# Two reorderings in a two-layer trunk: retention's rotary and gate items alternate, and the down projections scale the second half's residual rows in products four and five

## The chip, the cores and the metric

The kernel runs on one core of a Trainium2 chip. The metric is the device time of one execution in microseconds. An execution is also recorded by the hardware profiler; its rows give engine, source line, tiles, start and length of each instruction. PE is the matrix engine (TensorE), DVE the vector engine (VectorE), ACT ScalarE, POOL GpSimd, and SP the engine that only issues DMAs here.

## The reference

The input x has 1024 rows of 1024 numbers. Two layers follow each other, with different mixers, and only the structure matters here:

```python
for i in range(2):
    mod = (e @ ada_w[i] + ada_b[i])[:, None, :]
    sh1, sc1, g1, sh2, sc2, g2 = jnp.split(mod, 6, axis=-1)
    y = mixers[i](x * (1 + sc1) + sh1)        # layer 0: gated deltanet, layer 1: retention
    x = layer_norm(ALPHA * x + (1 + g1) * y, ln_g[i, 0], ln_b[i, 0])
    y = conv_ffn(x * (1 + sc2) + sh2, ...)    # (silu(conv(gate)) * up) @ w_down, width 2816
    x = layer_norm(ALPHA * x + (1 + g2) * y, ln_g[i, 1], ln_b[i, 1])
```

Retention projects h to q, k, v and a gate; q and k are rotated by position (rotary), v is mixed over chunks, and the result is multiplied by silu(gate). `layer_norm` is a standardisation and then `* ln_g + ln_b` by column; this last step is called "the gain" below.

## The kernel before, in words

**Numbers.** Each operand of a matmul is split into a rounded high part and a rest (`split`, lines 88 to 90: an ACT copy at L89, a DVE subtraction at L90), and each product is three matmuls: high by high and the two cross terms (L110 to L112, L285 to L287, L1163, L1437).

**Halves.** The 1024 rows are two halves of 512, each of four row tiles of 128 rows; columns are two halves of 512 as well. A row tile of 128x1024 is loaded by `load_row` (L280).

**Strassen.** The large projections use seven products of half-size blocks in place of eight. In the up direction (`strassen`, L1157) a list of *items* is worked through one after the other; each gives four output blocks to a `sink`. An item's weight blocks must be split by ACT and DVE (L89, L90) before PE reaches it. In the retention layer the items are gate items (`gate_item`, L1663: one ACT silu per block at L1667 and a DMA) and rotary items (`rope_item`, L1639: six DVE operations of 128x512 for each of two column halves, L1651 to L1656, and four DMAs on ACT's queue). Before the change the order is two gate items, eight rotary items, six gate items. The value projection (`ret_v`, L1685) comes next.

**Down projections.** `proj_gen` (L1274) makes the feed-forward's down projection, once in each layer. Its seven products p = 0 to 6 (A blocks 11, S1, S2, S4, 12, S3, 22) each have eleven steps of 12 matmuls, so some 30 us each. At each step the A block `ar` (L1270) and the B block (`Bw` or `Br`, L1303) come by SP's queue and are split (`ab`, `bb`).

**Residual rows.** The residual rows of the second FFN sum are `gain(standardised rows)`. The standardised rows lie in a DRAM scratch (`xs`), without the gain. For the first half `xload(0, t)` (L1348) loads a row tile at p = 2 and DVE applies the gain there. For the second half `gain_half` (L1339 to L1346) prepares the rows beforehand: SP loads a 128x512 piece (L1343), GpSimd multiplies it by ln_g and adds ln_b (two operations, L1345), and GpSimd's own queue stores it to a second scratch `xg` (L1346). There are eight such pieces for each down projection: four row tiles by two column halves. `xload(1, t)` (L280) then loads the four row tiles from `xg` in product five's hooks.

**Buffers.** `xload` and `gain_half` take their SBUF tiles from the same tag, "lane", which has four slots of 4 KB for each partition (L43); so does a rotary item's scratch, and the pieces of `bg_gain` (L393, L394), which applies the gain of another row set on GpSimd in the background. A slot is free again when the last reader of its tile is done. The first half's four row tiles are in these slots from p = 2 on, until `finish` (L1357 to L1361: scale, add, statistics) and `norm` (L1363 to L1382) are through. In layer 0 they are then standardised (L294), transposed (L266) for the next layer and stored to scratch (L370); in layer 1 they are multiplied by the final gain (L1377 to L1381) and stored to the output by SP (L1379, L1382). The second half goes the same way after product seven; in layer 0 its transposes are L421. Each row tile's `norm` has one tiny GpSimd operation, the power of -0.5 (L1368).

**Order.** The program text doesn't fix the order of instructions. A list scheduler with a model of durations places each operation and each buffer, from the dependencies and the order in which the generators yield; the result is one fixed sequence for each engine and each DMA queue, which runs in order on the chip. Background work such as `bg_gain` is put in where slots and engines are free.

Of the kernel before, what the change touches and what calls it, by code (L numbers as in the profile page):

```python
# [22 lines left out]
RH = 4  # L23
# [10 lines left out]
def trunk_kernel(ctx: ExitStack, tc, A):  # L34
# [47 lines left out]
    def hs(half):  # L82
        return slice(half * HALF, (half + 1) * HALF)
# [322 lines left out]

    def build_T(B, xts, scale, shift, tags):
        tags = dict(zip(("T1", "T2", "T3", "T4", "22"), tags))
        tags["12"] = tags["T1"]
        for nm in tags:  # L410
            B[nm] = [None] * 4

        def put(nm, k, src, eng=dve):
            t = two(tags[nm], F32R, nm)
            split(t[0], t[1], src, eng)
            B[nm][k] = t

        def load(f, tag):
            pt = mm_tile()
            for t in range(4):  # L420
                pe.transpose(pt[:, t * P:(t + 1) * P], xts[t][:, f * P:(f + 1) * P], ident)  # L421
            tmp = tl(tag, [P, HALF], name="bt")
            act.activation(tmp, pt, AF.Identity, bias=shift[:, f:f + 1], scale=scale[:, f:f + 1])
            return tmp

        raw = []
        for k, tg in enumerate((("qkv", "qkv"), ("qkv", "qkv"), ("t2", "t2"), ("t2", "ada"))):
            b12, b22 = load(k, tg[0]), load(4 + k, tg[1])
            put("12", k, b12, pool if BAL["b3"] & 1 << k else dve)
            put("22", k, b22, pool if BAL["b2"] & 1 << k else dve)  # L430
            raw.append((b12, b22))

        one = tl("S", [P, P], F32R, name="one")
        act.activation(one, ident, AF.Copy)

        def whole(b, k):
            pt = mm_tile()
            for i, x in enumerate(B[b][k]):
                pe.matmul(pt, one, x, start=(i == 0), stop=(i == 1))
            return pt  # L440

        def rest():
            for k in range(4):
                t1, b22 = raw[k]
                x11 = whole("11", k)
                dve.tensor_sub(b22, b22, t1)
                put("T3", k, b22, pool if BAL["b3"] & 1 << k else dve)
                dve.tensor_add(b22, b22, x11)
                put("T2", k, b22, pool if BAL["bT"] & 1 << k else dve)
                dve.tensor_sub(t1, t1, x11)  # L450
                put("T1", k, t1, pool if BAL["b1"] & 1 << k else dve)
                dve.tensor_sub(b22, whole("21", k), b22)
                put("T4", k, b22)

        return rest
# [701 lines left out]
    def strassen(hT0, xts, scale, shift, items, tags=("hTb", "hTb", "qkv", "qkv", "aux"), direct=False):  # L1157
        B = {"11": hT0[:4], "21": hT0[4:]}
        nblk = [0]
# [7 lines left out]
        def side(n, s):  # L1167
            out = []
            for u in items[n][:2]:
# [4 lines left out]
                for i, b in enumerate((("11", "21"), ("12", "22"))[s]):  # L1174
                    for k in range(4):
                        mm3(X, w, k + 4 * i, B[b][k], i == 0 and k == 0, i == 1 and k == 3)
                out.append(X)
# [96 lines left out]
    def proj_gen(nj, ablk, wsrc, slots, xsrc, G, final, ln_next, tag, ltags, dst, key, mm=pe.matmul, gate=None, gain=None):  # L1274
# [64 lines left out]
        def gain_half(n):  # L1339
            hf, rs = n // 4, slice(HALF + n % 4 * P, HALF + (n % 4 + 1) * P)  # L1340
            x = tl("lane", [P, HALF], name="xg")
            with after("w"):
                sp.dma_start(x, gain[1][rs, hs(hf)])  # L1343
            for r, op in zip(grows, (ALU.mult, ALU.add)):
                pool.tensor_tensor(x, x, r[hf], op)  # L1345
            pool.dma_start(xsrc[rs, hs(hf)], x)  # L1346
# [100 lines left out]
        for p, (an, bn, fin, side, fresh) in enumerate(prods):  # L1447
            if gate and p < 2 or banks[side] is None:
                banks[side] = acc4() if gate and p < 2 or side == 0 else [sc_tile(), sc_tile(), mm_tile(), mm_tile()]
                if gate and p == 1:  # L1450
                    banks[0] = banks[1]
                    banks[1] = None
            accs = banks[0] if gate and p == 1 else banks[side]
            tail = []
            depth = ltags[3] if p == 6 else 2
            for j in range(nj):
                if gate and p < 2:
                    yield gate(j)
                    yield from take("qkv", 2)
                    give("qkv", 2)  # L1460
                a, w = ops(an, bn, j, not gate and p < (7 if final else 5))
                with after("a"):
                    for st in steps[p * nj + j + ahead:p * nj + j + ahead + 1]:
                        load_b(*st)
                if gain and p < 2 and j % 2 == 0 and p * 4 + j // 2 < 8 and j < 8:
                    gain_half(p * 4 + j // 2)
                if gain and p == 2 and j % 2 == 0 and j < 8:
                    xload(0, j // 2)
                if p == 2 and j < 4 and gate:
                    xload(0, j)  # L1470
                    finish(0, j, 0, c11[j])
                if j >= nj - depth:
                    tail.append((j, a, w))
                else:
                    for t in range(4):
                        mma(accs[t], t, a, w, fresh and j == 0, False, mm if p < 2 else pe.matmul if fresh else mm_on)
                        yield 0.0
                for _ in range(-(-20 // (nj - 1)) if p == 6 else 4 if p == 5 else 2):
                    if later:
                        later.pop(0)()  # L1480
                if p == 5 and j > 1 and not later:
                    for _ in range(-(-16 // (nj - 2))):
                        if hooks:
                            hooks.pop(0)()
                bg_step()
            while later:
                later.pop(0)()
            if p == 5:
                while hooks:
                    hooks.pop(0)()  # L1490
            if p == 6:
                pin[0] = None
            for t in range(4):
                for j, a, w in tail:
                    mma(accs[t], t, a, w, fresh and j == 0, j == nj - 1, mm if p < 2 else pm_on if p == 6 else pe.matmul if fresh else mm_on)
                fin(t, accs[t])
                yield 0.0
            if p == 1:
                yield "P2"
            if p == 4:  # L1500
                hooks = [] if final else ln_hooks(0, xts[0], tag, ln_next, outs, dst, key, bal["h"])
                hooks += [lambda t=t: xload(1, t) for t in range(4)]
# [106 lines left out]
    def next0():  # L1609
        if not fbox:  # L1610
            while bg or pend:
                bg_step()
            fbox["f"] = fold(1, 0, 1)
        return fbox["f"]
# [24 lines left out]
    def rope_item(h, j):  # L1639
        def start():  # L1640
            c = {}

            def sink(q, a, b):
                c[q] = c_of(q, a, b)
                hf = q % 2
                if hf not in c or hf + 2 not in c:
                    return
                x1, x2 = c[hf], c[hf + 2]
                cos, sin = trig(h, j)
                m = tl("lane", [P, 2, HALF], name="rm")  # L1650
                dve.tensor_mul(m[:, 0], x2, sin[hf])  # L1651
                dve.tensor_mul(m[:, 1], x1, sin[hf])
                dve.tensor_mul(x1, x1, cos[hf])
                dve.tensor_mul(x2, x2, cos[hf])
                dve.tensor_sub(x1, x1, m[:, 0])
                dve.tensor_add(x2, x2, m[:, 1])  # L1656
                for d, x in enumerate((x1, x2)):
                    act.dma_start(qd[j, h, d][:, hs(hf)], x)
            return sink
        u = 8 * j + 2 * h  # L1660
        return A["ret_wqk"][u], A["ret_wqk"][u + 1], start, None

    def gate_item(u):  # L1663
        def start():
            def sink(q, a, b):
                c = c_of(q, a, b) if b is not None else tl("cv", [P, 516], name="sg")[:, 0:HALF]
                act.activation(c, a if b is None else c, AF.Silu)  # L1667
                act.dma_start(gd[u + q // 2][:, hs(q % 2)], c)
            return sink
        return A["ret_wg"][u], A["ret_wg"][u + 1], start, None  # L1670

    sc_r, sh_r = next0()
    B = strassen(h0, xts, sc_r, sh_r, [gate_item(0), gate_item(2)]
                 + [rope_item(h, j) for h in range(RH) for j in range(2)] + [gate_item(u) for u in range(4, 16, 2)], ("hTa", "aux", "qkv", "qkv", "hTa"), True)
    hT = [h0, []]
    xlo = []
    for t in range(4):
# [271 lines left out]
```

## Time and profile before

| | |
|---|---|
| median of 3 runs | 2971.46 us (2971.45 to 2976.05) |
| span of the profiled execution, first to last instruction | 2967.8 us |
| mean granted TensorE clock in it | 0.985 |
| PE, DVE, ACT, POOL busy | 2820.5, 2242.4, 1316.5, 474.8 us |
| layer 0's down projection | about 1200 to 1427 us |
| retention's items | about 1427 to 1745 us |
| layer 1's down projection | about 2731 to 2949 us, then normalising and output to 2967.8 |

The profiled execution's whole time is not shown beside its span; the span lies 3.66 us below the median of the runs. A row of a timeline reads: start in us, length in us, engine, line, operation, out<-in, tile and types, count, and in brackets how long the engine had been idle before and what ended that. In a table of stretches each engine's busy time stands with its instruction count in parentheses. A row of waits reads: engine, tile and line that waited, <- who ended the wait, then total us, number of times, and the longest.

### The profile page before, as it was taken

To read this page: it belongs to the slowest core of one execution; us is meant where nothing else is said; L and a number is where in the kernel's file an instruction comes from. 1 tells how busy PE (TensorE), PEld (TensorE's weight loads), DVE (VectorE), ACT (ScalarE), POOL (GpSimd) and SP (SyncE) were. 2 spreads that over 40 slices of the span, in tenths; PEclk is the share of its full clock that TensorE was granted. 3 is DMA by queue.
4 is the path that set the end of the run, shared out by engine and by line. 5 is a ranking of instruction groups with operands and counts; after the bars stand their busy time and mean duration, and the time that the engine had idled before them with its cause. 6 is when DMAs were issued, how large, how long until landed. Compare 5 with 4: busy or idle time off the path is not lost. (4 is left out here: it accounts for less than half of the span.)

```text
span 2967.8 us, 38939 instructions
## 1 busy us (share of the span) xinstructions
PE 2820.5 (95%) x13638; PEld 2304.5 (78%) x13638; DVE 2242.4 (76%) x4005; ACT 1316.5 (44%) x2413; POOL 474.8 (16%) x469
## 2 busy tenths in 40 slices
PE   8999898999999999999999999999999999999997
PEld 7887777887788888787877887777777788887786
DVE  5787787656688888879678645666689887777979
ACT  4744564444544444446433442222344544444443
POOL 0312221100001111610000202322202011112301
PEclk9999999999999999999999999999999999999998
DMA  7231222254245445865333544665664243335753
GB/s 275 79 113 65 86 79 79 83 167 160 91 158 163 158 151 174 305 198 179 120 128 117 181 160 152 203 189 175 205 212 157 91 135 107 107 107 176 274 183 137
DMA packets 244404, 451.01 MB, mean 152 GB/s; under 512 B 23088, under 2 KB 76592, under 8 KB 244208
## 3 DMA queue, kind: packets, MB, share of 16 engines
q1 hardware_dynamic: 213088, 401.07, 41.0%
q10 hardware_dynamic: 29760, 43.00, 4.0%
q0 software_dynamic: 1360, 4.46, 0.4%
q8 instruction: 107, 1.75, 0.3%
q14 instruction: 89, 0.73, 0.1%
HBM read 339.91 MB, written 108.53 MB: 151 GB/s over the span
## 5 line engine op out<-in xcount | busy, mean ns | idle before, releaser
L651 PE MATMUL acc<-hT,wh 128*128 128x512 f32 x960 | 299.3, 393 | 0.0
L1437 PE MATMUL acc<-bb,ab 128*128 128x512 f32 x984 | 231.4, 393 | 6.6 <-DVE bb L90 5.4
L1585 POOL TENSOR_TENSOR o<-o 128x512 f32<-128x512 f32 x80 | 110.7, 1394 | 716.4 <-DVE o L1578 490.8
L1437 PEld LDWEIGHTS acc<-bb,ab 128*128 128x128 f32 x984 | 182.6, 188 | 50.2 <-DVE bb L90 10.2
L1163 PE MATMUL acc<-T,wb 128*128 128x512 f32 x840 | 203.1, 391 | 6.7 <-DVE wb L90 6.7
L651 PEld LDWEIGHTS acc<-hT,wh 128*128 128x128 f32 x960 | 181.9, 190 | 34.1
L651 PE MATMUL acc<-hT,wl 128*128 128x512 f32 x480 | 201.1, 419 | 0.0
L89 ACT ACTIVATE ab<-ar 128x512 fp32r<-128x512 f32 x210 | 129.6, 625 | 152.7 <-PE mm L287 36.9
L90 DVE TENSOR_TENSOR ab<-ar,ab 128x512 fp32r<-128x512 f32 x210 | 161.9, 777 | 41.1 <-ACT ab L89 41.1
L1163 PEld LDWEIGHTS acc<-T,wb 128*128 128x128 f32 x840 | 157.0, 188 | 43.2 <-DVE wb L90 9.8
L90 DVE TENSOR_TENSOR wl<-wr,wh 128x1024 fp32r<-128x1024 f32 x95 | 119.7, 1260 | 69.6 <-ACT wh L89 68.6
L90 DVE TENSOR_TENSOR wb<-mm,wb 128x512 fp32r<-128x512 f32 x216 | 145.5, 682 | 31.2 <-ACT wb L89 30.6
L90 DVE TENSOR_TENSOR wb<-wr,wb 128x512 fp32r<-128x512 f32 x162 | 111.1, 691 | 69.8 <-ACT wb L89 69.1
L89 ACT ACTIVATE wh<-wr 128x1024 fp32r<-128x1024 f32 x95 | 100.7, 1061 | 132.3 <-PE acc L651 53.1
L1224 ACT ACTIVATE pc<-acc 128x512 f32<-128x512 f32 x143 | 84.9, 593 | 160.7 <-PE acc L1163 97.4
L1564 DVE SCALAR_TENSOR_TENSOR o<-g,vc,o 128x512 f32<-128x512 f32 (+2 forms) x176 | 145.4, 843 | 4.7 <-ACT o L1559 4.1
L89 ACT ACTIVATE wb<-mm 128x512 fp32r<-128x512 f32 x216 | 124.0, 595 | 51.9 <-DVE mm L1213 50.3
L89 ACT ACTIVATE wb<-wr 128x512 fp32r<-128x512 f32 x162 | 99.4, 628 | 104.0 <-DMA wr<-in_ffn_up 38.8
L651 PE MATMUL acc<-wh,hT 128*128 128x512 f32 x384 | 135.6, 415 | 1.6 <-DVE vv L90 1.6
L110 PE MATMUL acc<-T,wb 128*128 128x512 f32 x292 | 116.0, 397 | 9.4 <-DVE wb L90 9.4
L472 DVE SCALAR_TENSOR_TENSOR qkv<-raw,vc,qkv 128x512 f32<-128x512 f32 x144 | 111.6, 779 | 11.5 <-ACT qkv L470 10.7
L223 DVE SCALAR_TENSOR_TENSOR ada<-mvw,e,ada 128x512 f32<-128x512 f32 x140 | 106.9, 764 | 17.4 <-DMA mvw<-in_ada_w 17.1
(641 smaller groups left out, 7466.8 us busy)
## 6 DMA issues: line engine op xcount, KB each, us to landing
wr<-in_ffn_up SPq DMA_DIRECT2D x92, 512.0 KB, 4.4
mvw<-in_ada_w SPq DMA_DIRECT2D x80, 512.0 KB, 4.3
ad<-o SPq DMA_DIRECT2D x154, 256.0 KB, 3.1
ar<-ad SPq DMA_DIRECT2D x154, 256.0 KB, 3.9
Br<-in_ffn_down SPq DMA_DIRECT2D x88, 256.0 KB, 3.8
wr<-in_ret_wv SPq DMA_DIRECT2D x32, 512.0 KB, 3.9
ar<-od SPq DMA_DIRECT2D x56, 256.0 KB, 5.3
xs<-xt ACTq DMA_DIRECT2D x24, 512.0 KB, 3.7
```

The costliest lines, as they stand in the source:

```text
L89: act.activation(dst_h, src, AF.Copy)
L90: eng.tensor_tensor(dst_l, src, dst_h, ALU.subtract)
L110: mm(acc, wl[:, k], hl[0], start=first, stop=False)
L223: dve.scalar_tensor_tensor(a, wr[:, kk], e[:, k:k + 1], a, ALU.mult, ALU.add)
L472: dve.scalar_tensor_tensor(oh, raw[:, 3 - j:515 - j], w[:, 3 - j:4 - j], oh, ALU.mult, ALU.add)
L651: pq(pe.matmul(out, lhsT, rhs, start=start, stop=stop), cost)
L1163: return pe.matmul(*a, skip_group_check=True, **kw)
L1224: act.activation(t, X, AF.Copy)
L1437: return pe.matmul(*args, skip_group_check=True, **kw)
L1564: dve.scalar_tensor_tensor(tv, gv[:, c0 - j:c1 - j], w[:, 2 - j:3 - j], tv, ALU.mult, ALU.add)
L1585: (dve if fp == 0 else pool).tensor_tensor(o[d], o[x], o[y], op)
```

## The change

First, in `proj_gen`, `gain_half(0..7)` is called in the even steps of the products p = 3 and p = 4 (the fourth and fifth) and no longer in p = 0 and p = 1. Nothing in it is changed, nor its buffers. Second, retention's list of items is reordered: after gate items 0 and 2 comes a rotary item, a gate item, a rotary item and so on until the six remaining gate items are used; the last two rotary items follow each other at the end.

```diff
@@ proj_gen
-                if gain and p < 2 and j % 2 == 0 and p * 4 + j // 2 < 8 and j < 8:
-                    gain_half(p * 4 + j // 2)
+                if gain and p in (3, 4) and j % 2 == 0 and j < 8:
+                    gain_half((p - 3) * 4 + j // 2)
                 if gain and p == 2 and j % 2 == 0 and j < 8:
                     xload(0, j // 2)
@@ retention mixer
     sc_r, sh_r = next0()
+    ropes = [rope_item(h, j) for h in range(RH) for j in range(2)]
+    gates_ = [gate_item(u) for u in range(4, 16, 2)]
     B = strassen(h0, xts, sc_r, sh_r, [gate_item(0), gate_item(2)]
-                 + [rope_item(h, j) for h in range(RH) for j in range(2)] + [gate_item(u) for u in range(4, 16, 2)], ("hTa", "aux", "qkv", "qkv", "hTa"), True)
+                 + [it for pair in zip(ropes, gates_) for it in pair] + ropes[6:], ("hTa", "aux", "qkv", "qkv", "hTa"), True)
```

## The prediction, made before the changed kernel ran

> **What bounds the kernel now.** I read the page's head first, then the busy time by 10-us stretches, then what TensorE waited for.
>
> ```profile
> span 2967.8 us, 38939 instructions
> PE 2820.5 (95%) x13638; PEld 2304.5 (78%) x13638; DVE 2242.4 (76%) x4005; ACT 1316.5 (44%) x2413; POOL 474.8 (16%) x469
> ```
>
> TensorE is busy for 2820.5 of 2967.8 us. A change that adds no matmul can win only from the other 147 us, and it loses where it makes TensorE wait, or where it lengthens what follows the last matmul. So I looked at four places that the change touches: the start of both down projections, the end of each, and the rotary stage. The stretches at the two starts (columns: length, then busy us and instructions of PE, weight loads, DVE, ACT, POOL, then the granted clock, the DMA share, GB/s) and what PE waited for there:
>
> ```profile
> 1200.00:1210.00 10.00, 5.98 (x25) 4.30 (x24) 8.86 (x11) 8.00 (x21) 9.48 (x9) 1.00 1.05 392
> 1210.00:1220.00 10.00, 7.02 (x23) 5.06 (x22) 10.00 (x6) 2.73 (x6) 8.47 (x9) 0.83 1.05 395
> ...
> 2730.00:2740.00 10.00, 7.71 (x32) 5.69 (x32) 8.68 (x10) 6.90 (x13) 8.75 (x8) 1.00 1.03 374
> 2740.00:2750.00 10.00, 6.85 (x28) 4.72 (x26) 10.00 (x6) 3.81 (x7) 9.98 (x8) 1.00 1.05 401
> 2750.00:2760.00 10.00, 9.79 (x36) 7.95 (x37) 9.22 (x11) 0.93 (x2) 6.54 (x6) 0.83 1.03 383
> ```
> ```profile
> PE acc L285 <- DVE ab L90: 7.0, 4, 2.8
> ```
> ```profile
> PE acc L285 <- DVE ab L90: 4.9, 3, 2.6
> ```
>
> PE lacks 7.00 us of 20 in layer 0 (4.02 and 2.98) and 5.65 of 30 in layer 1 (2.29, 3.15, 0.21). Both waits name VectorE's operand split (L90). DVE and GpSimd are both nearly full there, and the DMA engines as well, with about 390 GB/s. Now the instructions themselves:
>
> ```profile
> 1207.47 6.78 DVE L90 TENSOR_TENSOR ab<-ar,ab 128x512 fp32r<-128x512 f32 x2
> ...
> 1218.54 0.68 DVE L90 TENSOR_TENSOR ab<-ar,ab 128x512 fp32r<-128x512 f32 x1
> ```
> ```profile
> 1211.21 2.49 POOL L1345 TENSOR_TENSOR xg<-xg,rowb 128x512 f32<-128x512 f32 x2
> ...
> 1215.48 2.50 POOL L1585 TENSOR_TENSOR o<-o 128x512 f32<-128x512 f32 x2
> ...
> 1222.32 14.47 POOL L1345 TENSOR_TENSOR xg<-xg,rowb 128x512 f32<-128x512 f32 x2 [3.82 <-DMA xg<-xs]
> ```
>
> Two splits take 6.78 us beside a full GpSimd, and one takes 0.68 us once GpSimd has paused. The other way round, two of the gain's operations take 14.47 us beside a full DVE, where two take 2.49 us otherwise. So the two engines hold each other up, and the gain (L1345) is one of the two jobs that fill GpSimd here. The other is L1585 of the last gate unit, which stays.
>
> **Part 1, the starts without the gain.** Products one and two lose 16 GpSimd operations, 8 loads and 8 stores per layer. At best the whole idle time goes: −7.00 and −5.65. At worst nothing does, since L1585 and the first A and B tiles stay, or it turns a little against us with another order. GpSimd works some 18 of the 20 us in layer 0, and two of L1585 take as long as two of the gain's (2.50 and 2.49). I take a bit over half: −4 and −3.5, together **−7.5** (bounds 0 and −12.65).
>
> **Part 1, where the gain goes.** The title says products four and five; the order of instructions says otherwise. Each gain tile needs a slot of "lane", which has four. From product three on all four hold the first half's residual rows (L1348), until these are normalised and stored. In both layers the order of after has the gain's GpSimd operations behind the first half's four L1368 and ahead of the second half's four. On SP the eight L1343 loads stand behind the first half's release, and the four L280 loads, which fetch the second half's rows from what the gain stored, behind its stores. So the gain is a serial chain between the halves: load, two operations, store, a second load in the same slot, two operations, store, and L280. On GpSimd alone it is at least this long:
>
> ```profile
> L1345 POOL TENSOR_TENSOR xg<-xg,rowb x32: 1257/1625/20702, 1199.6 to 2782.6; 128x512 f32<-128x512 f32 x32
> ```
> ```profile
> L1346 POOL DMA_DIRECT2D xg<-xg x16: 557/582/759, 1202.6 to 2784.5; - x16
> ...
> DMA to landing us min/median/max: 2.3/5.3/6.1
> ```
>
> 16 × 1.28 (an undisturbed one is 1.26 to 1.28) + 8 × 0.58 = 25.1 us of one in-order queue.
>
> *Layer 1.* Nothing follows this projection, so the chain lands at the end of the kernel. The rows of before there:
>
> ```profile
> 2932.79 0.33 SPq L1382 DMA_DIRECT2D out_dram<-xt  x1
> 2934.81 0.33 SPq L280 DMA_DIRECT2D xt<-xg  x1
> 2935.23 2.72 SPq L1382 DMA_DIRECT2D out_dram<-xt  x3
> 2939.26 1.65 SPq L280 DMA_DIRECT2D xt<-xg  x3
> ```
> ```profile
> 2944.15 0.69 DVE L1360 SCALAR_TENSOR_TENSOR xt<-xt,pa 128x512 f32<-128x512 f32 x1 [1.99 <-DMA xt<-xg]
> ...
> 2963.65 0.69 DVE L1381 TENSOR_TENSOR xt<-xt,rowb 128x512 f32<-128x512 f32 x1
> ```
> ```profile
> 2851.46 2.93 DMA Br<-in_ffn_down
> ...
> 2939.26 4.80 DMA xt<-xg
> ```
>
> The first slot comes free at 2934.8, when the first row tile's last store has landed (issued 2932.79; the L280 that takes its place in before goes out at 2934.81). A 256 KB load takes about 2.93 us (the Br row is of that size), so the gain starts near 2937.8 instead of long before. Its first tile: two operations to 2940.6, store issued by 2941.2, landed 2.5 to 2.8 us later (nearest to the minimum of 2.3, because the DMA engines are idle by then; median 5.3 under load) near 2944, second load there by 2946.7. Laid out in GpSimd's order of after (a1 a2, store a, b1 c1 b2 d1 c2 e1, store b, d2, store c, e2, store d, f1, store e, f2 g1 h1, store f, g2 h2, stores g and h) the last two stores are issued at about 2965 and 2965.5, against 2962.9 with no gap at all, and land near 2968.3. The last L280, 512 KB, takes 3.7 to 4.8 (4.80 for three at once; I take 4): 2972.3. Behind it stand on DVE 16 operations of 128x512 (0.60 us from start to start, 0.69 long) and 7 small ones: about 10.5 us. The last store's end comes 3.46 us after the last DVE operation (2967.8 − 2964.34). In all 2972.3 + 10.5 + 3.5 = 2986.3: **+18.5**. Lower bound +15 (no gap on GpSimd, store 2.3, load 3.7). Upper bound about +30: each of the three landings in series at the loaded figure, 5.3 for the stores, adds 2.5 to 3 each, and some gaps.
>
> *Layer 0.* The next layer's gate projections stand ready to cover it.
>
> ```profile
> 1399.20 2.06 SPq L280 DMA_DIRECT2D xt<-xg  x4
> ```
> ```profile
> 1403.35 23.89 PE L1437 MATMUL acc<-bb,ab 128*128 128x512 f32 x104 [0.60 <-DVE bb L90]
> ...
> 1437.96 1.04 PE L421 MATMUL mm<-cst,xt 128*128 128x128 f32 x8
> ...
> 1451.05 0.47 PE L110 MATMUL acc<-12_12989,wl 128*128 128x512 f32 x1
> ```
> ```profile
> 1431.60 0.81 DVE L294 TENSOR_SCALAR xt<-xt,mv 128x1024 f32<-128x1024 f32 x1 [0.73 <-POOL mv L1368]
> ...
> 1434.29 1.23 DVE L90 TENSOR_TENSOR wl<-wr,wh 128x1024 fp32r<-128x1024 f32 x1 [1.88 <-ACT wh L89]
> ...
> 1439.74 1.23 DVE L90 TENSOR_TENSOR wl<-wr,wh 128x1024 fp32r<-128x1024 f32 x1 [4.22 <-ACT wh L89]
> ```
>
> In before the second half's rows are ready at 1432.4 and first needed as operands at 1451.05: 18.6 us of cover. Now the first gain loads go out at 1399.2; the same 25 us of GpSimd and three landings make the L280 tiles arrive at about 1432, 1437, 1442 and 1442.5; in before they were issued at 1399.2. DVE's order of after puts the first two tiles' L1360 ahead of the third gate unit's weight split, the last two ahead of the fourth's. The splits that ran at 1434.29 and 1439.74 then come at about 1442 and 1449, and the units that need them were to start near 1438 and 1443.5. TensorE waits 4.3 us, then about 1.5 more, and the second half's rows are ready near 1453, against 1451 + 5.8. The first B blocks then follow with hardly a lead. I take **+7** (bounds 0, if the splits keep ahead, and +16, if the chain starts 9 us later, below).
>
> **Part 2, rotary and gate items alternate.**
>
> ```profile
> sum 260.00, PE 251.39 PEld 205.17 DVE 185.38 ACT 93.86 POOL 15.73; mean PE 9.67 PEld 7.89 DVE 7.13 ACT 3.61 POOL 0.61
> ```
> ```profile
> 1500.00:1510.00 10.00, 9.40 (x42) 7.47 (x41) 9.88 (x17) 3.50 (x7) 0.00 (x0) 1.00 0.43 133
> ...
> 1520.00:1530.00 10.00, 8.94 (x40) 7.09 (x39) 9.48 (x16) 3.78 (x7) 0.00 (x0) 1.00 0.14 53
> ...
> 1650.00:1660.00 10.00, 8.94 (x39) 7.08 (x39) 5.75 (x10) 2.97 (x6) 4.96 (x4) 1.00 0.99 317
> ...
> 1690.00:1700.00 10.00, 10.00 (x46) 8.29 (x45) 3.87 (x6) 3.50 (x6) 0.00 (x0) 1.00 0.43 153
> ```
> ```profile
> PE acc L1163 <- DVE wb L90: 5.3, 5, 1.1
> PE sc L1163 <- DVE wb L90: 2.7, 3, 1.1
> ```
>
> The first row sums 26 stretches of 10 us (1490 to 1750): 8.61 us of idle PE, all behind rotary items, none beside the gates (1690 has DVE at 3.87). Each rotary item ends with a burst of twelve DVE operations, and the next item's splits stand behind it: eight waits, 8.0 us, 0.6 at the first boundary and 1.06 at most later ones. Alternation does not shorten the burst, and it spills into the next item whatever that is. But in the order of after every boundary has the interleaving of the first one in before, so 8 × 0.6 = 4.8 remain: **−3.8** (bounds 0 and −8.6). The last two items are now rotary ones, so a burst, and the first six GpSimd gain operations of the mixer (in before hoisted to where 1650 shows GpSimd at 4.96), come beside the start of the value projection: **+1.5** (0 to +3).
>
> Sum on the execution of 2967.8: −7.5 + 18.5 + 7 − 3.8 + 1.5 = **+15.7**. The median of the runs is 2971.46, 3.66 above that span; so the forecast is **2987.2 us**, 0.53% slower.
>
> [...]
>
> **The rivals.**
> - *The relief outweighs the chain; not slower.* The whole of both starts (−12.65) and all the rotary waits (−8.6) go, layer 0's cover holds, and the tail costs its minimum: −21.3 + 15 = −6.3, 2965.2. It decides once layer 1's chain costs less than what is relieved. For it: DVE is named in every one of these waits. Against it: L1585 stays, and the burst is as long as before. Half-way cases lie within 0.2%.
> - *DVE starves the gain in layer 0.* If each L1345 takes 7.2 us (half of 14.47) while DVE is full, the gain stands until DVE falls idle, about 9 us later; layer 0 costs +16 and the total is +25: 2996; with loaded landings in the tail (+10) 3006. For it: the seventh product's own splits run there. Against it: in after DVE has nothing of the second half to do until the rows arrive.
> - *Alternation does nothing*, because each rotary burst costs the same 1.06: 2991.
> - *The gain does run in products four and five.* Then it is hidden, the total is −7.5 − 3.8 + 1.5: 2961.7. Against it stand the slots and the order; I give it 2%.
>
> **How the numbers follow.** A run of this kernel can tell about 0.2% (6 us) from no change. Forecast (own range 2978 to 2996) 53%, starved gain 18%, alternation without effect 14%, relief outweighing 13% (5 of it beyond 0.2%, 8 within), products four and five 2%. Of the first three, 3 more may fall within 0.2%. Faster 0.07, same 0.11, slower 0.82. The range, 2970 to 3004, leaves out the fast end and the loaded tail.
>
> **What would show it.** In the profile after: L1343 loads behind 2934 and GpSimd busy for some 25 us after them; a DVE gap of 20 us and more ahead of the last L1360 waits; PE at 9 or more of 10 in the first 20 us of each down projection; PE waits on weight splits behind layer 0's last product; waits of 0.6 rather than 1.06 after each rotary item. I am wrong if L1345 runs beside products four and five, if TensorE's idle time at the starts stays, or if the span ends less than 12 us after before's.

## The result, and the profile after

The changed kernel takes 2989.58 us (median of 4 runs, 2987.09 to 2992.01) against 2971.45 us, a ratio of 1.0062 with a 95% interval of 1.0051 to 1.0074: 0.6% slower. The forecast was 2987.2. The sum is near; its terms are not, and errors of opposite sign make it so. The experiments show that the kernel holds a gain of 0.5% that this version doesn't reach.

The head of the page after, and the two starts of the down projections in the same columns as before:

```profile
span 2985.3 us, 38928 instructions
PE 2825.0 (95%) x13638; PEld 2310.6 (77%) x13638; DVE 2219.1 (74%) x4005; ACT 1316.3 (44%) x2413; POOL 442.8 (15%) x469
```
```profile
1200.00:1210.00 10.00, 10.00 (x45) 8.26 (x44) 10.00 (x16) 8.96 (x23) 3.59 (x3) 1.00 1.05 395
1210.00:1220.00 10.00, 10.00 (x46) 8.28 (x45) 10.00 (x14) 4.52 (x8) 2.40 (x2) 1.00 1.05 389
...
2730.00:2740.00 10.00, 10.00 (x45) 8.15 (x44) 4.79 (x8) 4.01 (x8) 0.00 (x0) 1.00 0.75 257
2740.00:2750.00 10.00, 9.48 (x42) 7.51 (x42) 10.00 (x13) 6.95 (x13) 4.70 (x3) 1.00 1.05 398
2750.00:2760.00 10.00, 10.00 (x46) 8.29 (x45) 10.00 (x16) 4.62 (x8) 1.77 (x1) 1.00 1.05 392
```

TensorE, which lacked 7.00 and 5.65 us there, lacks 0 and 0.52. GpSimd is down from 17.95 to 5.99 us in layer 0's 20 us. DVE does more than before (14 operations in 1210 to 1220 and 13 in 2740 to 2750, 6 in each of them before), and in layer 0 the DMA engines carry as much as before (395 and 389 GB/s against 392 and 395; in layer 1 257, 398 and 392 against 374, 401 and 383). This part of the change does what one would hope.

What it costs stands where product seven ends in layer 0, and behind product seven in layer 1. First TensorE, then DVE, in layer 0:

```profile
1391.92 23.87 PE L1437 MATMUL acc<-bb,ab 128*128 128x512 f32 x104 [0.60 <-DVE bb L90]
1425.47 0.79 PE L110 MATMUL acc<-hT,wl 128*128 128x512 f32 x1 [9.68 <-DVE xt L1360]
```
```profile
1423.24 1.57 DVE L1360 SCALAR_TENSOR_TENSOR xt<-xt,pa 128x512 f32<-128x512 f32 x1 [4.39 <-DMA xt<-xg]
1424.74 0.67 DVE L1360 SCALAR_TENSOR_TENSOR xt<-xt,acc 128x512 f32<-128x512 f32 x1
```

TensorE stands still for 9.68 us until the second L1360 has read a PSUM accumulator (`acc`). That one stands in DVE's order behind the first L1360, which waits for the second half's residual row from `xg`. The gate unit's first matmul needs the accumulator. In before the same L1360 ran at 1420.01, seven microseconds ahead of the end of product seven. Now the tail of layer 1 (GpSimd, DVE, and the chain of waits):

```profile
2935.87 2.66 POOL L1345 TENSOR_TENSOR xg<-xg,rowb 128x512 f32<-128x512 f32 x2 [13.77 <-DMA out_dram<-xt]
...
2960.63 1.09 POOL L1346 DMA_DIRECT2D xg<-xg  x2
```
```profile
2946.71 0.70 DVE L1358 TENSOR_TENSOR acc<-acc,rowb 128x512 f32<-128x512 f32 x1 [3.38 <-PE acc L1437]
2959.58 1.67 DVE L1360 SCALAR_TENSOR_TENSOR xt<-xt,pa 128x512 f32<-128x512 f32 x1 [12.17 <-POOL xg L1345]
...
2980.62 1.28 DVE L1381 TENSOR_TENSOR xt<-xt,rowb 128x512 f32<-128x512 f32 x2
```
```profile
2796.33 29.92 PE acc L1437 x132
...
2932.84 3.36 DMA out_dram<-xt
...
2960.33 3.82 DMA xt<-xg
```

The gain's sixteen operations and eight stores run from 2935.87 to 2961.72, between the halves, 25.9 us; the page's chain goes from the first half's output over these to the load of the second half's rows.

**The ledger.** The same matmuls in both executions, by their start (ends where said), show where the time went. Each column is one execution:

| point on TensorE | before | after | shift |
|---|---|---|---|
| first L285 of layer 0's down projection | 1198.71 | 1197.40 | -1.31 |
| its first L1437 | 1268.45 | 1257.38 | -11.07 |
| end of product seven | 1427.24 | 1415.79 | -11.45 |
| L110 that waits for `wl`, first B blocks | 1467.77 | 1470.18 | +2.41 |
| last run of twelve L1163 of retention's items | 1755.45 | 1753.08 | -2.37 |
| last L112 of layer 1's up projection | 2729.39 | 2735.20 | +5.81 |
| last L287 of its down projection | 2887.73 | 2885.70 | -2.03 |
| end of the last matmul | 2949.07 | 2946.68 | -2.39 |
| end of the span | 2967.8 | 2985.3 | +17.5 |

So the starts give 9.8 and 7.8, the end of layer 0 costs 13.9, the items give 4.8, the way from there to layer 1's down projection costs 8.2, and the tail 19.9.

### The profile page after: what moved, and what is told of

It is laid out like the page before. It is cut to its first block, busy times and chain, and to the rows that moved or that the text cites. A ratio compares the mean times of both kernels' runs of the same rounds, so it can differ in the third digit from the quotient of the medians.

```text
span 2985.3 us, 38928 instructions
## 1 busy us (share of the span) xinstructions
PE 2825.0 (95%) x13638; PEld 2310.6 (77%) x13638; DVE 2219.1 (74%) x4005; ACT 1316.3 (44%) x2413; POOL 442.8 (15%) x469
## 4 chain that ended last, share of the span: by engine, by line
PE 71%; DVE 11%; DMA 8%; ACT 4%; issue 3%; POOL 2%; SPq 0%; ACTq 0%; DVEq 0%; POOLq 0%
PE acc L651 14%; PE acc L1163 10%; PE acc L110 6%; PE acc L111 5%; PE acc L112 5%; PE sc L1163 5%; PE sc L651 3%; PE mm L651 2%; PE acc L1437 2%; PE sc L111 2%; PE sc L110 2%; PE sc L112 2%; DMA op<-od 1%; DVE bb L90 1%; PE mm L654 1%
## 5 line engine op out<-in xcount | busy, mean ns | idle before, releaser
L1437 PE MATMUL acc<-bb,ab 128*128 128x512 f32 x984 | 232.8, 394 | 6.1 <-DVE bb L90 5.4
L1585 POOL TENSOR_TENSOR o<-o 128x512 f32<-128x512 f32 x80 | 112.8, 1420 | 792.8 <-DVE o L1578 493.9
L1437 PEld LDWEIGHTS acc<-bb,ab 128*128 128x128 f32 x984 | 183.9, 189 | 49.8 <-DVE bb L90 10.1
L1163 PE MATMUL acc<-T,wb 128*128 128x512 f32 x840 | 202.8, 390 | 3.4 <-DVE wb L90 3.4
L90 DVE TENSOR_TENSOR ab<-ar,ab 128x512 fp32r<-128x512 f32 x210 | 152.5, 731 | 51.4 <-ACT ab L89 51.3
L1163 PEld LDWEIGHTS acc<-T,wb 128*128 128x128 f32 x840 | 157.1, 188 | 39.4 <-DVE wb L90 6.5
L110 PE MATMUL acc<-T,wb 128*128 128x512 f32 x292 | 115.9, 397 | 9.4 <-DVE wb L90 9.4
```

Of the source, the lines that this page charges most:

```text
L90: eng.tensor_tensor(dst_l, src, dst_h, ALU.subtract)
L110: mm(acc, wl[:, k], hl[0], start=first, stop=False)
L1163: return pe.matmul(*a, skip_group_check=True, **kw)
L1437: return pe.matmul(*args, skip_group_check=True, **kw)
L1585: (dve if fp == 0 else pool).tensor_tensor(o[d], o[x], o[y], op)
```

## The experiments

All are compared with the kernel before, on the same chip.

**e1, the gain alone.** Only the hunk in `proj_gen`; retention's list as before.

> Only the gain is moved; retention's items stay in the order of before. Theory (the two reorderings add up, each in its own stage, as the shifts of TensorE between the two traces say): starts of the down projections -9.8 and -7.8, end of layer 0's +13.9, tail of layer 1 +19.9, so +16 us, about 2987. Rival (the alternation makes the loss, the gain is worth what it seems): 2971 or below.

Measured: 2988.97 us, ratio 1.0056 (1.0044 to 1.0068), +16.7. The loss is the gain's, and the parts add up. TensorE waits 10.19 us for L1360 there, at the same place.

**e2, the alternation alone.** Only the hunk in the retention mixer.

> Only retention's items alternate; the gain stays in products one and two. Theory: seven waits of 0.60 us in place of eight of 0.60 to 1.06 give -4.5 us, the start of the value projection takes 5.5 back, so +1 to +3 us, about 2973. Rival (the stage's relief stays, the 5.5 us came from layer 0's late end): -4.5, about 2967.

Measured: 2971.09 us, ratio 0.9998 (0.9990 to 1.0007): no difference. The waits of TensorE in the items are all alike, as the forecast had it, here the first and the last of the seven:

```profile
1504.33 3.02 PE L1163 MATMUL sc<-T,wb 128*128 128x512 f32 x12 [0.61 <-DVE wb L90]
...
1738.23 3.02 PE L1163 MATMUL sc<-T,wb 128*128 128x512 f32 x12 [0.61 <-DVE wb L90]
```

Seven times 0.61 is 4.3 in place of 8.61, and with the last item TensorE is 8.93 us ahead of before, 4.6 of them from the items. Up to layer 1's down projection it loses 8.2 (to -0.69), and 6.2 of that between the matmuls that before starts at 1756.35 and 1799.81, at the start of the value projection. On the same stretch every kernel with the alternation loses 5.9 to 8.9 us, and the four without it (e1, e7, e9, e10) at most 0.25. So more is given back there than was won among the items. Both guesses of the expectation missed by 2 to 4 us.

**e3, buffers of its own.** The whole change, and two buffers for the gain:

```diff
-    BUFS = {..., "xT": 4}
+    BUFS = {..., "xT": 4, "gx": 2}
-            x = tl("lane", [P, HALF], name="xg")
+            x = tl("gx", [P, HALF], name="xg")
```

> The whole change, but gain_half takes two buffers of its own in place of lane slots; then the order has the gain truly in products four and five. Theory (the lane slots alone push the gain behind the first half): both ends lose nothing, both starts win 17.6, the retention stage gives +1 to +3, so -14 to -17 us, about 2955. Rival (sixteen GpSimd operations beside a full VectorE cost the same stalls in products four and five): the 17.6 come back there, 2968 or more.

Measured: 2971.5 us, ratio 0.9993 (0.9980 to 1.0007). Both ends are as good as in before (the slots were what pushed the gain there), and the gain does run away from them: p = 3 and 4 of the text have their GpSimd operations at 1257.4 to 1316.4 us, while TensorE, which comes later than the text's steps, is at products three and four (they start at 1256.1 and 1286.0). But a new stall of 13.19 us stands ahead of the first matmul of product five. By time the rival won; its reason had still to be tried.

**e5, meant to take a load out of the way.** As e3, and `with after(("out", 0)):` around the rotary tables' loads.

> As e3 (own buffers for the gain, so it runs in products four and five), but the rotary tables' loads (L1632), which stood in SP's queue of product four waiting for buffers that the gain's rows hold, are ordered behind layer 0's output. The eight L1343 stay in SP's queue. Theory (e3's 13.2 us stall of TensorE in product four is SP standing at L1632 and L1343 while the B loads wait behind): with one of the two holds gone the stall falls below 9 us, the time to 2955 to 2966. Rival (GpSimd and VectorE hold each other up in product four): stall near 13 us, 2970 or more.

Measured: 2971.28 us, 0.9991 (0.9979 to 1.0004), stall 15.01. The edit missed its aim: the tables' loads (L1633 here) stayed in SP's queue where they were, so e5 is e3 again and tells nothing between the theories. Its profile tells more. SP's queue, then DVE and TensorE:

```profile
1301.23 0.33 SPq L1303 DMA_DIRECT2D Br<-in_ffn_down  x1
1307.26 0.32 SPq L1343 DMA_DIRECT2D xg<-xs  x1
...
1309.12 0.46 SPq L1303 DMA_DIRECT2D Br<-in_ffn_down  x1
1312.19 0.32 SPq L1343 DMA_DIRECT2D xg<-xs  x1
...
1313.55 0.38 SPq L1270 DMA_DIRECT2D ar<-ad  x1
1317.74 0.33 SPq L1633 DMA_DIRECT2D trig<-in_trig  x1
1318.16 0.38 SPq L1303 DMA_DIRECT2D Br<-in_ffn_down  x1
```
```profile
1321.27 0.69 DVE L1317 TENSOR_TENSOR Br<-Bw,Br 128x512 f32<-128x512 f32 x1 [15.09 <-DMA Br<-in_ffn_down]
```
```profile
1332.01 0.76 PE L285 MATMUL sc<-bb,ab 128*128 128x512 f32 x1 [15.01 <-DVE u L1410]
```

SP issues in order and stands for 5.7, 2.6 and 3.8 us: twice at a gain load whose buffer is still being stored, once at a table whose buffer (tag "auh") the gain's rows hold until GpSimd is done. The B block waits behind them, DVE waits 15.09 us for the B block, and L1410, which frees a PSUM bank, stands behind that on DVE. GpSimd and DVE aren't in each other's way there: DVE is idle.

**e6, as e5, and the gain's loads on GpSimd's queue.**

```diff
-            with after("w"):
-                sp.dma_start(x, gain[1][rs, hs(hf)])
+            pool.dma_start(x, gain[1][rs, hs(hf)])
```

> As e5, and the gain's loads are issued by GpSimd's own queue in place of SP's, so nothing of the gain can hold SP's queue. Theory (SP's queue): no stall over 1 us in products four and five, both starts free, about -15 us, 2957. Rival (the engines): GpSimd has as much work beside VectorE as in e3 and more, stall near 13 us, 2970 or more.

Measured: 2969.57 us, 0.9984 (0.9974 to 0.9993). No stall at that place, but not for the reason expected: without an order against the weights' loads the scheduler put the gain ahead of all of the up projection's GpSimd work, from 766 us on, where it works beside the transposes of the normalised rows and TensorE loses 8.2 us (between the matmuls that before starts at 753.6 and 829.0). A miss as a test of the queue.

**e9, four buffers.** Retention as before; the gain in products four and five, with a tag that is idle at that time.

```diff
-            x = tl("lane", [P, HALF], name="xg")
+            x = tl("xT", [P, HALF], name="xg")
```

> Retention's items as before; the gain in products four and five with four buffers of its own (those of the tag xT, idle at that time) in place of two, loads on SP's queue. With four, a load waits for a store that was issued a whole product earlier. Theory (SP stood 5.7 and 2.6 us at L1343 and 3.8 us at the rotary tables' loads in e5, and the B loads behind them came late): only the 3.8 are left, TensorE's stall in product four at most 6 us, the time about 2959. Rival (sixteen GpSimd operations beside VectorE): the stall stays at 13 to 15 us, 2970.

Measured: 2962.93 us, 0.9966 (0.9954 to 0.9978). The stall is 6.75 us, just above the bound, and SP stands once for long in its queue, 5.5 us at the tables:

```profile
1306.13 0.32 SPq L1270 DMA_DIRECT2D ar<-ad  x1
1311.98 0.33 SPq L1632 DMA_DIRECT2D trig<-in_trig  x1
1312.40 0.38 SPq L1303 DMA_DIRECT2D Br<-in_ffn_down  x1
```
```profile
1326.57 0.77 PE L285 MATMUL sc<-bb,ab 128*128 128x512 f32 x1 [6.75 <-DVE u L1410]
```

**e10, and the tables on GpSimd's queue.**

```diff
-                    sp.dma_start(t[hf], (A["trig"][i] if j else A["trigq"][h, i])[:, hs(hf)])
+                    pool.dma_start(t[hf], (A["trig"][i] if j else A["trigq"][h, i])[:, hs(hf)])
```

> As e9, and the rotary tables are loaded by GpSimd's queue, so that nothing of the gain or of its row buffers can hold SP's queue in products four and five. Theory: no stall over 1 us there, both starts free, both ends as before, -15 us, about 2956. Rival (the engines): stall of 13 us, 2970.

Measured: 2957.68 us, 0.9947 (0.9935 to 0.9960), -15.4. The stall is down to 2.24 us; the same sixteen GpSimd operations run there, at 1261.0 to 1307.4 us. So the queue was the main cause, and the rival falls: 13 to 15 us with both kinds of holds, 6.75 with one, 2.24 with none. The expectation had less than 1 us; what the 2.24 are wasn't tried.

```profile
1320.35 0.51 PE L285 MATMUL sc<-bb,ab 128*128 128x512 f32 x1 [2.24 <-DVE u L1410]
```

**e4, the gain in product two alone**, with lane slots and the alternation:

```diff
+                if gain and p == 1 and j < 8:
+                    gain_half(j)
```

> The whole change, but gain_half's eight calls stand in product two alone, with lane slots. Theory (the stall at the start comes from GpSimd doing the gain and the last gate unit's L1585 at the same time, and from no lead of the splits yet): 2957 to 2961. Rival (it is any GpSimd work beside a full VectorE, whenever it comes): 7 us of TensorE idle time stand in product two, about 2972.

Measured: 2959.63 us, 0.9960 (0.9947 to 0.9972). In layer 0 TensorE lacks 1.54 us in product two, where DVE is full, and 1.96 more in product three (by the wait at 1285.70), all behind DVE's splits; it lacked 7.00 in before:

```profile
1220.00:1230.00 10.00, 10.00 (x46) 8.29 (x45) 4.93 (x4) 2.53 (x5) 9.89 (x8) 1.00 0.72 229
1230.00:1240.00 10.00, 8.46 (x36) 6.16 (x35) 10.00 (x10) 6.96 (x13) 5.62 (x7) 1.00 1.04 397
```

The gain's sixteen operations take from 1223.1 to 1270.6 us here, three of them 11.19 us beside a full DVE, where one takes 1.30 by the median, so the two engines hold each other up here too. It costs half of before's idle time. Whether that is so because the splits have a lead by then or because the last gate unit's L1585 is past, this run doesn't separate.

**e7, no gain operations** (the rows keep their loads and stores, and the kernel leaves ln_g and ln_b out of them):

```diff
-            for r, op in zip(grows, (ALU.mult, ALU.add)):
-                pool.tensor_tensor(x, x, r[hf], op)
```

> The kernel before without GpSimd's two operations for each gain tile: the loads and stores of the gain stay where they were, but the second half's residual rows keep neither ln_g nor ln_b (left out of the computation). Theory (the stall at the start of the down projections is GpSimd beside VectorE): TensorE's idle time in layer 0's first 20 us falls from 7.0 to below 1.5, in all about -14 us, 2958. Rival (it is the DMA traffic, near 390 GB/s there): idle time of 5 us or more, 2967 or more.

Measured: 2952.91 us, 0.9928 (0.9915 to 0.9941). The same DMA traffic, and the idle time falls from 7.00 to 1.66, a little above the 1.5 expected:

```profile
1200.00:1210.00 10.00, 8.34 (x37) 6.60 (x36) 10.00 (x16) 6.39 (x18) 3.94 (x4) 1.00 1.03 392
1210.00:1220.00 10.00, 10.00 (x46) 8.29 (x45) 7.92 (x10) 4.57 (x9) 3.74 (x3) 1.00 1.05 394
```

So the stall at the start is GpSimd beside DVE, and not the 390 GB/s. The time falls by 20.9 us, more than the 14 expected.

**e8, a gate item last.** Three rotary items in a row, then gate and rotary in turn.

```diff
-  [gate_item(0), gate_item(2)] + [rope_item(h, j) for h in range(RH) for j in range(2)] + [gate_item(u) for u in range(4, 16, 2)]
+  [gate_item(0), gate_item(2)] + ropes[:2] + [it for pair in zip(ropes[2:], gates_) for it in pair]
```

> The gain as before; retention's items in the order gate 0, gate 2, three rotary items, then gate and rotary in turn, so that a gate item is the last and a rotary item the last but one. Theory (in e2 the alternation won 5 us among the items and lost as much after them, because the last two rotary items keep VectorE, the lane slots and SP's qd loads busy when the value projection starts): -3 to -4 among the items, a loss of 0 to 1.5 behind them, about 2968.5. Rival (the loss behind the items comes with any alternation, through the later start of bg_gain): 2971 or more.

Measured: 2973.19 us, 1.0002 (0.9993 to 1.0012). The theory falls: 7.9 us are lost between the matmuls of 1756.35 and 1799.81, so that loss doesn't hang on which of the two is last.

**e11, the rotary scratch in a buffer of its own.**

```diff
-                m = tl("lane", [P, 2, HALF], name="rm")
+                m = tl("rmx", [P, 2, HALF], name="rm")
```

> As e2 (only the alternation), but the rotary items' scratch has a buffer of its own, so that lane slots are free during the items and the first three pieces of bg_gain are ordered earlier. Theory (what the alternation wins among the items is lost behind them because bg_gain's first pieces come beside the start of the value projection): -2 to -4, about 2968.5. Rival (the loss comes with the qd loads and the residual rows' loads behind them in SP's queue, which stand as in e2): 2971.

Measured: 2968.78 us, 0.9990 (0.9981 to 1.0000), -4.3 by the medians. The waits among the items vanish but for one of 2.68 us in the last (I had expected only `bg_gain` to move), and two stretches behind them have together the least of TensorE of all kernels, 32.88 us of 40:

```profile
1735.00:1755.00 20.00, 17.32 (x70) 13.79 (x69) 16.72 (x17) 4.62 (x7) 9.90 (x7) 0.91 0.87 272
1755.00:1775.00 20.00, 15.56 (x59) 12.41 (x58) 13.21 (x11) 3.08 (x3) 7.21 (x5) 0.83 0.88 301
```

The time is near the theory's, but by the gain among the items and not by its reason: 8.9 us are still lost behind them.

**e12, e10 and e11 together.**

> e10 and e11 together: the gain in products four and five with four own buffers and the rotary tables on GpSimd's queue, and the alternation with the rotary scratch in a buffer of its own. Theory (the two add up): -15 and -3, about 2955. Rival (the alternation's win is given back at the value projection whatever else changes): as e10, 2958, or above it where the tables on GpSimd's queue come beside the alternating items.

Measured: 2957.01 us, 0.9944 (0.9929 to 0.9959). As e10; the alternation adds nothing that can be told. This and e10 are faster than both kernels of the case.

## Why the prediction came out

**That the gain does not run in products four and five** was right: the slots hold it until the first half is through, and with other buffers (e3, e9, e10) the ends cost nothing. Had the change done what it says, with free queues, it would be worth about 15 us (e10 -15.4, e12 -15.6).

**The tail: +18.5 forecast, +19.9 measured.** The chain was right up to its last load. The projection ended 2.39 us earlier than in before, so the forecast's times are to be taken 2.4 earlier: the gain began at 2935.87 (2935.4), and the last L280 landed at 2969.76 (2969.9), with the last store issued 2 us sooner than laid out and 4.3 us in landing in place of 2.8. From there the forecast had DVE wait for that load and then work 10.5 us. DVE was still at the earlier rows and came to the last pair of L1360 at 2971.46; its last operation ended at 2981.9 (2980.4). The DVE gap of 20 us and more that was to show the chain wasn't there: four L1358 split it, and the longest part is 12.17.

**The starts: -7.5 forecast, -17.6 measured. This step was mis-sized.** I let L1585 keep half of the stall, since its operations are as long. But GpSimd alone, without the gain, is busy for 5.99 of 20 us, and DVE works between. Also, I priced idle time by itself only. Layer 0's 7.00 us of idle time came with a shift of 9.76, and some 1.6 us of the difference is the clock: eight matmuls behind the gap of 2.51 us start 0.20 us further apart than those around them. The stretches of before, 5 us each, last three columns granted clock, DMA share, GB/s:

```profile
1210.00:1215.00 5.00, 2.49 (x10) 1.73 (x9) 5.00 (x2) 1.67 (x3) 4.98 (x6) 0.94 1.05 405
1215.00:1220.00 5.00, 4.54 (x15) 3.33 (x14) 5.00 (x5) 1.06 (x3) 3.50 (x4) 0.72 1.05 385
1220.00:1225.00 5.00, 5.00 (x24) 4.10 (x23) 5.00 (x9) 1.66 (x4) 2.68 (x1) 1.00 1.05 399
```

At 0.72 fifteen matmuls take 4.54 us, where 24 fit into 5.00 at 1.00. The eight, from 1214.31 to 1217.44 us, start 0.43 us apart (the first two 0.57), and those before and after them 0.23. Behind the longest gap here, 2.82 us up to 1208.76, the granted clock from 1205 to 1210 is 1.00, and the matmuls start 0.23 to 0.24 us apart (the first two 0.33). So here the length of one gap doesn't tell whether the clock falls behind it; what does isn't shown.

**The end of layer 0: +7 forecast, +13.9 measured, by another wait.** The forecast had TensorE wait for the third and fourth gate unit's weight splits, behind DVE's waiting L1360, near 1438. It waited at once, at the first gate unit, for the PSUM accumulators that product seven had filled and that the same waiting DVE had not read. I looked only at the operands of the next matmuls, and not at the banks they write to. The gap of 9.68 us and the slower matmuls behind it (eight that start 0.43 us apart, the first two 0.59, and 0.23 from the ninth on) shift the same matmuls by 11.55 us (-11.45 to +0.10); the rest of the 13.9 comes later, with smaller waits (0.92 and 0.83 in after). The granted clock is 0.56 in the stretch around the gap's end.

```profile
1420.00:1430.00 10.00, 4.53 (x13) 3.63 (x14) 6.17 (x11) 0.00 (x0) 7.03 (x8) 0.56 0.77 258
```

**The items: -3.8 forecast, -4.8 measured.** Seven waits of 0.60, as the orders had said; an eighth falls away, as no item follows the last. **What comes behind them: +1.5 forecast (0 to +3), 5.9 measured** between the matmuls of 1756.35 and 1799.81, and 8.2 in the ledger's long row, of which a part lies further on, where e1, e9 and e10 with the old order lose 3.5, 3.2 and 0.3 as well. The place was named right, the price was put at a fourth. In e2, where the alternation stands alone, TensorE waits there 2.6 us for loads of `xlo` (rows of the second half that L266's matmuls transpose), 0.9 for DVE's splits and 0.8 for ACT's copy of a transpose, and runs at a granted clock of 0.83 from 1775 to 1785, which is worth 1.7; together 6.0 of the 6.2. The last of these loads in SP's queue, first in before, then in e2, and the wait in e2:

```profile
1763.63 0.32 SPq L1681 DMA_DIRECT2D xlo<-xs  x1
```
```profile
1771.64 0.38 SPq L1683 DMA_DIRECT2D xlo<-xs  x1
```
```profile
1776.15 0.44 PE L266 MATMUL mm<-cst,xlo 128*128 128x128 f32 x2 [2.20 <-DMA xlo<-xs]
```

In e2 these loads stand among those of `bg_gain`'s pieces (L384, L387). The first twelve operations of these pieces run on GpSimd at 1641 to 1672 us in before, beside gate items, and at 1756 to 1785 in e2. In e8 and e11 they run at 1727 to 1770 and 1732 to 1764, TensorE waits mostly for other things, and 7.9 and 8.9 us are lost. No run alternates and leaves the pieces where before had them, so that they are the cause is not shown, and the point stays open.

So the total was right by luck: the relief of the starts and of the items was 10.1 and 1.0 us larger than put, and the costs at the end of layer 0, behind the items (the ledger's row) and in the tail 6.9, 6.7 and 1.4 larger; the ledger's other rows give 2.0 back. Of the rivals, the starved gain was partly seen: in layer 0 the first six operations took 13.16 us beside DVE's splits where 7.51 is their time in the tail. The four L280 landed at 1423.1, 1428.0, 1433.5 and 1435.7, which is 2.5 to 4.6 us later than laid out once the projection's shift of 11.45 is taken off. With +13.9 the end of layer 0 is nearer to this rival's +16 than to the +7, though TensorE's long wait was for another thing than either had.

```profile
1390.46 13.16 POOL L1345 TENSOR_TENSOR xg<-xg,rowb 128x512 f32<-128x512 f32 x6 [23.42 <-PE acc L1437]
...
2939.45 7.51 POOL L1345 TENSOR_TENSOR xg<-xg,rowb 128x512 f32<-128x512 f32 x6
```

## What to carry to other kernels

Before moving background work to a quieter place, ask which buffers it takes and who holds them there: a move in the text may end up behind the holder, at the end of the kernel. With buffers of its own, look at the queue that issues its loads: loads that wait for their buffers hold the later loads of that queue (in e5 SP stood 5.7, 2.6 and 3.8 us, and TensorE 15.01), and the cure here was enough buffers (e9, 6.75) and another queue (e10, 2.24). And when an engine's in-order stream is made to wait, price what it frees (PSUM banks, slots) as well as what it computes: the accumulators that DVE had not read held TensorE for 9.68 us here.

## What the runs showed of the hardware

- Idle time of TensorE cost more than itself: 7.00 us of gaps came with a shift of 9.76 (before against after; granted clock 0.72 from 1215 to 1220 us), 9.68 us in one gap with 11.55 (after; 0.56 from 1420 to 1430), and 15.01 us in one gap with 17.4 (e5, by the shift of the same matmuls ahead of it and behind it, -11.45 to +5.97).
- One L1345 operation on GpSimd took 20.70 us (before, from 1252.13), where the shortest took 1.26. DVE was busy for 20.34 us of that time, with 34 operations, none of them longer than 1.35 us; so the operation lasted far longer than any one of DVE's. What held it so long isn't shown.
